# A heads' third key tile: its softmax weights turned by VectorE through DRAM instead of by TensorE, and half of the weight loads issued by ScalarE

## The chip, the cores and the metric

The kernel runs on one core of a Trainium2 chip. The core has a matrix engine (TensorE, "PE" in the profile, with its weight loads as "PEld"), VectorE ("DVE"), ScalarE ("ACT"), GpSimd ("POOL") and SyncE ("SP"), which here mostly issues DMA transfers. Each engine works through an instruction list of its own; semaphores order them against each other. The metric is device time in microseconds (us), the median of several executions.

## The reference

One layer of a hybrid decoder: 512 positions, 2048 channels, float32. An RMS-normalised input goes through one input projection `W_in`, whose columns feed three token mixers: A, dilated attention of 8 heads; B, a gated causal convolution with a layer norm; C, banded attention of 16 query heads. Their outputs side by side go through `W_out` and are added to the input. A second normalisation and a SwiGLU network follow. The part that the change touches is the softmax-weighted sum of A. Cut to what matters:

```
s = einsum(q, k) * hd**-0.5          # per head, key, query; masked
p = exp(s - m);  denom = sum(p)      # softmax weights
o = einsum(p, v) / denom             # weights times values
mix = softmax over three patterns' log-sum-exp, times o
out = concat(a, b, c) @ W_out + x
```

The scores have queries on partitions; the sum over keys wants the keys there. So the weights `p` must be turned (transposed) between the two matmuls.

## The kernel before, in words

**Projections in units.** `W_in` and `W_out` are worked off in 95 units of 1024 x 128 weights: units 0 to 62 are `W_in`, 63 to 94 `W_out`. A unit arrives by DMA (512 KB, tile `w`), is split by ScalarE into a rounded high part (`wh`, L295) and by VectorE into the rest (`wl`, L269), and TensorE forms three products for each of eight steps, 24 matmuls of 128x512: high by high, high by low, low by high (L328 to L330). `SPLIT_BUFS` = 3 pairs of high and low exist; the split runs `SPLIT_AHEAD` = 2 units ahead of use.

**Raw buffers and loads.** `pump` (L237) issues the load of the next unit as soon as a raw buffer is free; units 51 to 90 use five buffers, since others hold the turned softmax weights. The load overwrites a buffer whose last reader was the subtraction `wl` of an earlier unit. While `cooling` is on (the input projection), a buffer is released a unit later than its last reader is emitted; after that a load is emitted right behind the `wl` that frees its buffer. All these loads go through SyncE's queue, except the first four.

**Order of work.** It is written out: the kernel is scheduled by hand, so each engine does its instructions in the order in which the program emits them. Between the projection's matmuls a clock of ticks (`Ticks`, a few matmuls each) calls the steps that fell due: scores, exponentials, turns, weighing, taps of the convolution (L590), layer norm sums (`lns`, split into `lnh` and `lnl`, then averaged by TensorE as `lnm`, L617 and L618) and so on. The ticks are the same for both ways of turning.

**An A head.** TensorE writes the scores into three PSUM banks `a..s`; ScalarE scales them by the query norm (L941), VectorE adds the bias and takes the maxima (L946), ScalarE exponentiates (`a..e`, L954). Eight of the ten 128x128 blocks of weights (of key tiles 0, 1 and 3) are turned in 32x32 pieces by VectorE (`blocks_turn`, L971, tile `z`), written to DRAM (`ed`), read back rearranged (`et`, four transfers), and split into a high part (`ph`, ScalarE, L993) and a low part (`pl`, VectorE, L999). The blocks of the third key tile are turned by TensorE (`flip`, L1006) into a PSUM bank, and split from there (L1012, L1017). `weigh` then multiplies by the values. There are eight heads, named a0 to a3 with a 0 or 1 behind the tile's name; a0 and a1 are worked during the input projection, a2 and a3 during `W_out`.

Of the kernel before, what the change touches and what calls it, by code (L numbers as in the profile page):

```python
# [60 lines left out]
SPLIT_BUFS = 3  # L61
X_AHEAD = 8
SPLIT_AHEAD = 2
WARM = 8


# [55 lines left out]
def kernel(ctx: ExitStack, tc: tile.TileContext, xT, wi, wo, wgu, wd, cst_in, outT):  # L122
# [20 lines left out]
    def slot(name, dt=F32, cols=T):  # L143
        return sp.tile([P, cols], dt, name=name, tag="s")
# [96 lines left out]
    def pump(limit, most=99, eng=nc.sync):  # L241
        while at["entry"] < len(entries) and len(raws) < limit and entries[at["entry"]][0] not in held and most:
            most -= 1
            buf, key, parts = entries[at["entry"]]
            size = [part.shape[-1] * (part.shape[1] if len(part.shape) == 3 else 1) for part in parts]
            t, o = take(buf, key, sum(size)), 0
            for part, n in zip(parts, size):
                to = t[:, o:o + n]
                eng.dma_start(to.rearrange("p (n f) -> p n f", n=part.shape[1]) if len(part.shape) == 3 else to, part)
                o += n  # L250
            at["entry"] += 1

# [563 lines left out]
    def attention(kind, box, mix, mi, heads):  # L816
# [34 lines left out]
        def head(h):  # L851
# [104 lines left out]

            ph, pl = {}, {}

            def block(i, j):
                for u, un in enumerate(us):  # L960
                    for ii, k0, n, o in un:
                        if ii == i:
                            f = o + j * P - k0
                            return es[u][:, f:f + P]

            def blocks_turn():
                z = wp.tile([P, 1024], F32, name=f"{name}z{h}", tag=f"raw{TURN_BUFS[0]}", bufs=1)
                to = z.rearrange("p (j b q) -> p b j q", j=4, b=8)
                for u, c, bs in ((0, slice(0, 2), slice(0, 2)), (0, slice(2, 3), slice(4, 5)), (1, slice(0, 2), slice(2, 6, 3)),
                                 (2, slice(0, 2), slice(3, 7, 3)), (2, slice(3, 4), slice(7, 8))):  # L970
                    nc.vector.transpose(to[:, bs], es[u].rearrange("p (b j q) -> p b j q", b=NT, j=4)[:, c])  # L971
                ticks.after(2, blocks_leave, z)

            def blocks_leave(z):
                d = tc.dram_tile([P, 1024], F32, name=f"{name}ed{h}")
                nc.sync.dma_start(d, z)
                ticks.after(3, blocks_back, d)

            def blocks_back(d):
                turned[0] = 3 - turned[0]  # L980
                t = wp.tile([P, 1024], F32, name=f"{name}et{h}", tag=f"raw{TURN_BUFS[turned[0]]}", bufs=1)
                for j in range(4):
                    nc.sync.dma_start(t[32 * j:32 * j + 32].rearrange("p (i c) -> p i c", i=4),
                                      d.rearrange("(i p) c -> p i c", i=4)[:, :, j * 2 * P:(j + 1) * 2 * P])
                ticks.after(5, blocks_high, t.rearrange("p (i b q) -> p b i q", i=4, b=8))

            def queries4(t):
                return t.rearrange("p (b i q) -> p b i q", b=NT, i=4)

            def blocks_high(src):  # L990
                for t in range(2):
                    ph[t] = slot(f"{name}ph{h}{t}", F32R)
                    nc.scalar.copy(queries4(ph[t]), src[:, NT * t:NT * t + NT])  # L993
                ticks.after(EV, blocks_low, src)

            def blocks_low(src):
                for t in range(2):
                    pl[t] = slot(f"{name}pl{h}{t}", F32R)
                    nc.vector.tensor_sub(queries4(pl[t]), src[:, NT * t:NT * t + NT], queries4(ph[t]).bitcast(F32))  # L999

            def flip(t):
                b = bank(f"{name}t{h}{t}")
                o = 0
                for j, i0, i1 in TBANKS[kind][t]:
                    for i in range(i0, i1 + 1):
                        nc.tensor.transpose(b[:, o:o + P], block(i, j), ident)  # L1006
                        o += P
                ticks.after(ev, high, t, b, o)

            def high(t, b, o):  # L1010
                ph[t] = slot(f"{name}ph{h}{t}", F32R)
                nc.scalar.copy(ph[t][:, :o], b[:, :o])  # L1012
                ticks.after(EV, low, t, b, o)

            def low(t, b, o):
                pl[t] = slot(f"{name}pl{h}{t}", F32R)
                nc.vector.tensor_sub(pl[t][:, :o], b[:, :o], ph[t][:, :o].bitcast(F32))  # L1017

            def weigh():
                b = bank(f"{name}o{h}")  # L1020
# [41 lines left out]
            if kind == "c":  # L1062
                ticks.after(tu, packed_exps)
                ticks.after(tu + s2, packed_norm)
                ticks.after(tu + 1, packed_turn)
            else:
                ticks.after(tu + s2, invert, h, den)
                ticks.after(tu + 2, blocks_turn)
                ticks.after(tu + s2 + fl + 2, flip, 2)
            ticks.after(t0 + at_v, weigh)  # L1070
            if h == 1:
                ticks.after(t0 + at_v - 2, sums_back)
# [720 lines left out]
```

## Time and profile before

| | us |
|---|---|
| median of 3 runs | 1826.89 (1826.79 to 1827.04) |
| the profiled execution's own time | 1827.03 |
| its span | 1825.3 |
| TensorE busy in the span | 1818.3 |
| VectorE, ScalarE, GpSimd busy | 1434.5, 1327.6, 1022.1 |
| input projection and mixers | 0 to 375 of the span |
| `W_out` | 375 to 562 |
| SwiGLU up and down | 562 to 1825 |

The profile's clock runs from the span's start; rows of a timeline give start and duration. Granted TensorE clock is 0.999. Busy times of matmuls overlap (each row's end is modelled), so what a matmul costs is read from the distance between starts. A row's bracket gives the engine's idle time before it and what ended that. A DMA row on SP or ACT is the issue alone.

### The profile page before, as it was taken

What the parts mean: (1) busy time and instruction counts of PE and PEld (TensorE: products, weight loads), DVE (VectorE), ACT (ScalarE), POOL (GpSimd) and SP (SyncE); (2) the same over time, 40 slices, a digit from 0 to 9 for tenths busy, and PEclk for the clock granted to TensorE, in tenths of its full rate; (3) what the DMA queues carried; (4) which work ended last, traced back from release to release, by engine and by line L of the source; (5) the groups of instructions that cost most, each with busy time, mean ns of one, the idle gap of its engine ahead of it and who ended that gap; (6) DMA issues with size and microseconds to landing.
All of it is one profiled execution on the core that took longest, in us unless ns stands there. A gap on an engine that the chain in (4) does not pass through costs nothing.

```text
span 1825.3 us, 26570 instructions
## 1 busy us (share of the span) xinstructions
PE 1818.3 (100%) x8191; PEld 1509.9 (83%) x8191; DVE 1434.5 (79%) x1996; ACT 1327.6 (73%) x1848; POOL 1022.1 (56%) x793
## 2 busy tenths in 40 slices
PE   9999999999999999999999999999999999999998
PEld 7888888888888888888888888888888888888887
DVE  6779999987689777777777777777777777777777
ACT  6345656664468778888888888888887778877775
POOL 0116555120014577786887868878775568775652
PEclk9999999999999999999999999999999999999999
DMA  7355456666343557787777877778687579877645
GB/s 279 96 161 157 152 172 182 195 211 214 130 145 113 130 142 206 191 222 192 194 205 191 220 192 197 204 190 223 176 278 261 195 230 293 259 256 255 231 127 105
DMA packets 409295, 354.61 MB, mean 194 GB/s; under 512 B 177088, under 2 KB 331840, under 8 KB 409152
## 3 DMA queue, kind: packets, MB, share of 16 engines
q1 hardware_dynamic: 408576, 352.12, 65.7%
q8 instruction: 65, 1.06, 0.2%
q10 hardware_dynamic: 576, 0.79, 0.1%
q14 instruction: 78, 0.64, 0.1%
HBM read 270.00 MB, written 74.41 MB: 189 GB/s over the span
## 4 chain that ended last, share of the span: by engine, by line
PE 99%; DVE 1%; DMA 0%; issue 0%; ACT 0%; SPq 0%; DVEq 0%; ACTq 0%
PE out L1374 15%; PE out L1375 15%; PE out L1372 15%; PE out L1637 7%; PE out L1639 7%; PE out L1638 7%; PE o L328 3%; PE o L330 3%; PE o L329 3%; PE cq L328 2%; PE cq L329 2%; PE cq L330 2%; PE ak L328 1%; PE aq L328 1%; PE av L328 1%; PE ak L330 1%
## 5 line engine op out<-in xcount | busy, mean ns | idle before, releaser
L1372 PE MATMUL out<-wh,h 128*128 128x512 f32 x1232 | 479.2, 389 | 0.0
L1374 PE MATMUL out<-wl,h 128*128 128x512 f32 x1232 | 479.2, 389 | 0.0
L1375 PE MATMUL out<-wh,h 128*128 128x512 f32 x1232 | 479.2, 389 | 0.0
L1372 PEld LDWEIGHTS out<-wh,h 128*128 128x128 f32 x1232 | 231.2, 188 | 48.1
L1374 PEld LDWEIGHTS out<-wl,h 128*128 128x128 f32 x1232 | 231.2, 188 | 48.1
L1375 PEld LDWEIGHTS out<-wh,h 128*128 128x128 f32 x1232 | 231.2, 188 | 47.9
L1637 PE MATMUL out<-wh,a 128*128 128x512 f32 x620 | 240.4, 388 | 0.0
L1638 PE MATMUL out<-wl,a 128*128 128x512 f32 x620 | 240.3, 388 | 0.0
L1639 PE MATMUL out<-wh,a 128*128 128x512 f32 x620 | 240.3, 388 | 0.0
L295 ACT CAST wh<-w 128x1024 fp32r<-128x1024 f32 (+2 forms) x94 | 97.0, 1032 | 115.8 <-PE o L329 48.9
L1647 DVE TENSOR_TENSOR y<-y,out 128x512 f32<-128x512 f32 x192 | 128.6, 684 | 47.6 <-PE out L1639 46.1
L269 DVE TENSOR_TENSOR wl<-w,wh 128x1024 fp32r<-128x1024 f32 (+2 forms) x95 | 114.1, 1203 | 30.0 <-ACT wh L295 28.9
L1639 PEld LDWEIGHTS out<-wh,a 128*128 128x128 f32 x620 | 116.4, 188 | 24.0
L1638 PEld LDWEIGHTS out<-wl,a 128*128 128x128 f32 x620 | 116.4, 188 | 23.8
L1637 PEld LDWEIGHTS out<-wh,a 128*128 128x128 f32 x620 | 116.4, 188 | 23.8
L590 DVE SCALAR_TENSOR_TENSOR y<-bu,cst,y 128x511 f32<-128x511 f32 (+14 forms) x120 | 89.8, 748 | 0.5
L328 PE MATMUL o<-mh_c,wh 128*128 128x512 f32 x128 | 50.3, 393 | 0.0
L328 PE MATMUL cq<-hh,wh 128*128 128x512 f32 x128 | 50.0, 391 | 0.0
L329 PE MATMUL cq<-hl,wh 128*128 128x512 f32 x128 | 49.9, 390 | 0.0
L329 PE MATMUL o<-ml_c,wh 128*128 128x512 f32 x128 | 49.9, 390 | 0.0
L330 PE MATMUL o<-mh_c,wl 128*128 128x512 f32 x128 | 49.9, 390 | 0.0
L330 PE MATMUL cq<-hh,wl 128*128 128x512 f32 x128 | 49.8, 389 | 0.0
(2359 smaller groups left out, 4736.4 us busy)
## 6 DMA issues: line engine op xcount, KB each, us to landing
od<-a SPq DMA_DIRECT2D x154, 256.0 KB
a<-od SPq DMA_DIRECT2D x154, 256.0 KB
w<-in_wi SPq DMA_DIRECT2D x58, 512.0 KB
w<-in_wo SPq DMA_DIRECT2D x32, 512.0 KB
x<-in_xT SPq DMA_DIRECT2D x16, 256.0 KB
xr<-in_xT SPq DMA_DIRECT2D x16, 256.0 KB
x2d<-xr SPq DMA_DIRECT2D x16, 256.0 KB
z<-x2d SPq DMA_DIRECT2D x64, 64.0 KB
```

The source lines that it names most:

```text
L269: fn(*args)
L295: (nc.vector.tensor_copy if u == 0 else nc.scalar.copy)(hi[:, :n], t[:, :n])
L328: nc.tensor.matmul(out, wh, xh, start=start, stop=False)
L329: nc.tensor.matmul(out, wh, xl, start=False, stop=False)
L330: nc.tensor.matmul(out, wl, xh, start=False, stop=stop)
L1372: nc.tensor.matmul(b, x[:, high], wh[:, s], start=c == f == 0 and q in (7, 1, 5, 2), stop=False, skip_group_check=True)
L1374: nc.tensor.matmul(b, x[:, high], wl[:, s], start=False, stop=False, skip_group_check=True)
L1375: nc.tensor.matmul(b, x[:, low], wh[:, s], start=False, stop=c == f == 1, skip_group_check=True)
L1637: nc.tensor.matmul(b[:, lo:hi], x[:, high], wh[:, s], start=start, stop=False, skip_group_check=True)
L1638: nc.tensor.matmul(b[:, lo:hi], x[:, high], wl[:, s], start=False, stop=False, skip_group_check=True)
L1639: nc.tensor.matmul(b[:, lo:hi], x[:, low], wh[:, s], start=False, stop=last, skip_group_check=True)
L1647: getattr(eng, op)(t, t, src)
```

## The change

It does two things.

First, in A heads the third key tile's two blocks take the same way as the other eight: VectorE turns them into a second tile `z2`, SyncE writes it to DRAM (`ec`, 128 KB) and reads it back by four transfers (`eu`, 32 KB each), and `blocks_high` and `blocks_low` split three sources instead of two. TensorE's transposes (`flip`) and the split from PSUM (`high`, `low`) are gone. The ticks of the remaining steps stay.

Second, the loads of units 46 to 94 are issued by ScalarE's queue (`nc.scalar`) instead of SyncE's, at the same places of the program.

```diff
--- before.py
+++ after.py
@@ -61,6 +61,7 @@
 SPLIT_BUFS = 3
 X_AHEAD = 8
 SPLIT_AHEAD = 2
+ACT_LOADS = 46
 WARM = 8
 
 
@@ -246,7 +247,8 @@
             t, o = take(buf, key, sum(size)), 0
             for part, n in zip(parts, size):
                 to = t[:, o:o + n]
-                eng.dma_start(to.rearrange("p (n f) -> p n f", n=part.shape[1]) if len(part.shape) == 3 else to, part)
+                by = nc.scalar if isinstance(key, int) and key >= ACT_LOADS else eng
+                by.dma_start(to.rearrange("p (n f) -> p n f", n=part.shape[1]) if len(part.shape) == 3 else to, part)
                 o += n
             at["entry"] += 1
 
@@ -956,65 +958,52 @@
 
             ph, pl = {}, {}
 
-            def block(i, j):
-                for u, un in enumerate(us):
-                    for ii, k0, n, o in un:
-                        if ii == i:
-                            f = o + j * P - k0
-                            return es[u][:, f:f + P]
-
             def blocks_turn():
                 z = wp.tile([P, 1024], F32, name=f"{name}z{h}", tag=f"raw{TURN_BUFS[0]}", bufs=1)
                 to = z.rearrange("p (j b q) -> p b j q", j=4, b=8)
                 for u, c, bs in ((0, slice(0, 2), slice(0, 2)), (0, slice(2, 3), slice(4, 5)), (1, slice(0, 2), slice(2, 6, 3)),
                                  (2, slice(0, 2), slice(3, 7, 3)), (2, slice(3, 4), slice(7, 8))):
                     nc.vector.transpose(to[:, bs], es[u].rearrange("p (b j q) -> p b j q", b=NT, j=4)[:, c])
-                ticks.after(2, blocks_leave, z)
-
-            def blocks_leave(z):
+                z2 = slot(f"{name}z{h}", cols=2 * P)
+                to = z2.rearrange("p (j b q) -> p b j q", j=4, b=2)
+                for n in range(2):
+                    nc.vector.transpose(to[:, n], es[n + 1][:, 2 * P:3 * P].rearrange("p (j q) -> p j q", j=4))
+                es.clear()
+                ticks.after(2, blocks_leave, z, z2)
+
+            def blocks_leave(z, z2):
                 d = tc.dram_tile([P, 1024], F32, name=f"{name}ed{h}")
                 nc.sync.dma_start(d, z)
-                ticks.after(3, blocks_back, d)
-
-            def blocks_back(d):
+                d2 = tc.dram_tile([P, 2 * P], F32, name=f"{name}ec{h}")
+                nc.sync.dma_start(d2, z2)
+                ticks.after(3, blocks_back, d, d2)
+
+            def blocks_back(d, d2):
                 turned[0] = 3 - turned[0]
                 t = wp.tile([P, 1024], F32, name=f"{name}et{h}", tag=f"raw{TURN_BUFS[turned[0]]}", bufs=1)
                 for j in range(4):
                     nc.sync.dma_start(t[32 * j:32 * j + 32].rearrange("p (i c) -> p i c", i=4),
                                       d.rearrange("(i p) c -> p i c", i=4)[:, :, j * 2 * P:(j + 1) * 2 * P])
-                ticks.after(5, blocks_high, t.rearrange("p (i b q) -> p b i q", i=4, b=8))
-
-            def queries4(t):
-                return t.rearrange("p (b i q) -> p b i q", b=NT, i=4)
-
-            def blocks_high(src):
-                for t in range(2):
+                t2 = slot(f"{name}eu{h}", cols=2 * P)
+                for j in range(4):
+                    nc.sync.dma_start(t2[32 * j:32 * j + 32].rearrange("p (i c) -> p i c", i=4),
+                                      d2.rearrange("(i p) c -> p i c", i=4)[:, :, j * 64:(j + 1) * 64])
+                b8 = t.rearrange("p (i b q) -> p b i q", i=4, b=8)
+                ticks.after(5, blocks_high, (b8[:, :NT], b8[:, NT:], t2.rearrange("p (i b q) -> p b i q", i=4, b=2)))
+
+            def by_query(t, src):
+                return t[:, :src.shape[1] * P].rearrange("p (b i q) -> p b i q", i=4, q=32)
+
+            def blocks_high(srcs):
+                for t, src in enumerate(srcs):
                     ph[t] = slot(f"{name}ph{h}{t}", F32R)
-                    nc.scalar.copy(queries4(ph[t]), src[:, NT * t:NT * t + NT])
-                ticks.after(EV, blocks_low, src)
-
-            def blocks_low(src):
-                for t in range(2):
+                    nc.scalar.copy(by_query(ph[t], src), src)
+                ticks.after(EV, blocks_low, srcs)
+
+            def blocks_low(srcs):
+                for t, src in enumerate(srcs):
                     pl[t] = slot(f"{name}pl{h}{t}", F32R)
-                    nc.vector.tensor_sub(queries4(pl[t]), src[:, NT * t:NT * t + NT], queries4(ph[t]).bitcast(F32))
-
-            def flip(t):
-                b = bank(f"{name}t{h}{t}")
-                o = 0
-                for j, i0, i1 in TBANKS[kind][t]:
-                    for i in range(i0, i1 + 1):
-                        nc.tensor.transpose(b[:, o:o + P], block(i, j), ident)
-                        o += P
-                ticks.after(ev, high, t, b, o)
-
-            def high(t, b, o):
-                ph[t] = slot(f"{name}ph{h}{t}", F32R)
-                nc.scalar.copy(ph[t][:, :o], b[:, :o])
-                ticks.after(EV, low, t, b, o)
-
-            def low(t, b, o):
-                pl[t] = slot(f"{name}pl{h}{t}", F32R)
-                nc.vector.tensor_sub(pl[t][:, :o], b[:, :o], ph[t][:, :o].bitcast(F32))
+                    nc.vector.tensor_sub(by_query(pl[t], src), src, by_query(ph[t], src).bitcast(F32))
 
             def weigh():
                 b = bank(f"{name}o{h}")
@@ -1066,7 +1055,6 @@
             else:
                 ticks.after(tu + s2, invert, h, den)
                 ticks.after(tu + 2, blocks_turn)
-                ticks.after(tu + s2 + fl + 2, flip, 2)
             ticks.after(t0 + at_v, weigh)
             if h == 1:
                 ticks.after(t0 + at_v - 2, sums_back)
```

How this moves instructions, at the places of which the prediction speaks. In the change, lines 251 to 958 stand two lower on the page than before (L295 is now L297), and those from 1020 on eleven or twelve higher up (L1085 is now L1073). ScalarE's list around the cast of unit 66, before (`wh66` is the cast of unit 66, `a2s` the scaling of scores, `a2e` an exponential, `mh_a0` the high part of a finished head):

```order
L295 CAST wh66_4390<-w66_4111 128x1024
L954 ACTIVATE a2e02_4399,a2d0_4001<-a2s02_4333,a2d0_4001 128x512
L941 ACTIVATE a2s10_4401<-a2s10_4401,aq2r_4232 128x128
L941 ACTIVATE a2s10_4401<-a2s10_4401,aq2r_4232 128x256
L941 ACTIVATE a2s11_4432<-a2s11_4432,aq2r_4232 128x384
L295 CAST wh67_4449<-w67_4183 128x1024
L954 ACTIVATE a2e10_4459,a2d1_4002<-a2s10_4401,a2d1_4002 128x128
L954 ACTIVATE a2e10_4459,a2d1_4002<-a2s10_4401,a2d1_4002 128x256
L941 ACTIVATE a2s12_4463<-a2s12_4463,aq2r_4232 128x512
L954 ACTIVATE a2e11_4483,a2d1_4002<-a2s11_4432,a2d1_4002 128x384
L1085 CAST mh_a0_4486<-mix_a0_3827 128x512
```

And with the change:

```order
L251 DMA w70_4416<-in_wo 128x1024
L297 CAST wh66_4418<-w66_4135 128x1024
L956 ACTIVATE a2e02_4427,a2d0_4021<-a2s02_4361,a2d0_4021 128x512
L943 ACTIVATE a2s10_4429<-a2s10_4429,aq2r_4260 128x128
L943 ACTIVATE a2s10_4429<-a2s10_4429,aq2r_4260 128x256
L943 ACTIVATE a2s11_4463<-a2s11_4463,aq2r_4260 128x384
L251 DMA w71_4478<-in_wo 128x1024
L297 CAST wh67_4480<-w67_4209 128x1024
L956 ACTIVATE a2e10_4490,a2d1_4022<-a2s10_4429,a2d1_4022 128x128
L956 ACTIVATE a2e10_4490,a2d1_4022<-a2s10_4429,a2d1_4022 128x256
L943 ACTIVATE a2s12_4494<-a2s12_4494,aq2r_4260 128x512
L956 ACTIVATE a2e11_4516,a2d1_4022<-a2s11_4463,a2d1_4022 128x384
```

The loads of units 70 and 71 now stand ahead of the casts of 66 and 67, and everything on ScalarE stands behind them.

VectorE's list from the subtraction of unit 65 to that of unit 66 with the change (`a2z0` are the turned weights of one head; L966 is L971 of the kernel before):

```order
L271 TENSOR_TENSOR wl65_4349<-w65_4055,wh65_4348 128x1024
L1154 TENSOR_TENSOR xr0_4341<-xr0_4341,o0_0_4345 128x512
L830 RECIPROCAL weights_sums1_564<-a2d0_4021 128x4
L966 STREAM_TRANSPOSE a2z0_4452<-a2e00_4357 128x2x4x32
L966 STREAM_TRANSPOSE a2z0_4452<-a2e00_4357 128x4x32
L966 STREAM_TRANSPOSE a2z0_4452<-a2e01_4387 128x2x4x32
L966 STREAM_TRANSPOSE a2z0_4452<-a2e02_4427 128x2x4x32
L966 STREAM_TRANSPOSE a2z0_4452<-a2e02_4427 128x4x32
L970 STREAM_TRANSPOSE a2z0_4458<-a2e01_4387 128x4x32
L970 STREAM_TRANSPOSE a2z0_4458<-a2e02_4427 128x4x32
```

The two L970 rows, into a second tile of the same name, are new; the other rows stood there in this order.

ScalarE's list from the cast of unit 74 to the layer norm's `lnh`, before:

```order
L295 CAST wh74_4905<-w74_4642 128x1024
L1012 CAST a3ph12_4924<-a3t12_4914 128x256
L295 CAST wh75_4959<-w75_4716 128x1024
L609 CAST lnh_4969<-lns_4932 128x512
L993 CAST a3ph10_4974<-a3et1_4890 128x512
```

And with the change:

```order
L251 DMA w78_4962<-in_wo 128x1024
L297 CAST wh74_4964<-w74_4687 128x1024
L251 DMA w79_5009<-in_wo 128x1024
L297 CAST wh75_5011<-w75_4757 128x1024
L611 CAST lnh_5021<-lns_4986 128x512
L1000 CAST a3ph10_5026<-a3et1_4944 128x512
L1000 CAST a3ph11_5028<-a3et1_4944 128x512
L1000 CAST a3ph12_5030<-a3eu1_4949 128x256
```

The copy `a3ph12` from PSUM has gone behind the two others, and the loads of units 78 and 79 stand ahead of the casts of 74 and 75.

## The prediction

> **What bounds the kernel now.** I read the page's busy times and chain first, then TensorE's waits, then the stretch of the changed work on each engine.
>
> ```profile
> PE 1818.3 (100%) x8191; PEld 1509.9 (83%) x8191; DVE 1434.5 (79%) x1996; ACT 1327.6 (73%) x1848; POOL 1022.1 (56%) x793
> PE 99%; DVE 1%; DMA 0%; issue 0%; ACT 0%; SPq 0%; DVEq 0%; ACTq 0%
> PE idle L354 <- DVE nhalf L360: 1.1, 1, 1.1
> PE sides L1602 <- DVE y L1616: 1.1, 2, 0.6
> ```
>
> TensorE (PE) is the chain, and waits 2.2 us in all, none of it here. So the change can win only what its removed matmuls cost on PE, and can lose whatever newly makes PE wait. The profiled execution took 1827.03 us: span 1825.3 and 1.7 around it, 0.14 above the median 1826.89. 0.2% is 3.65 us, about what a measurement can tell from no change.
>
> **The removed transposes.** Each head loses two PE transposes, sixteen in all.
>
> ```profile
> 315.83 0.38 PE L1006 MATMUL a0t<-ident,a0e 128*128 128x128 f32 x2
> 315.97 0.47 PE L328 MATMUL ak<-hh,wh 128*128 128x512 f32 x1
> 316.29 0.39 PE L329 MATMUL ak<-hl,wh 128*128 128x512 f32 x1
> 316.51 0.40 PE L330 MATMUL ak<-hh,wl 128*128 128x512 f32 x1
> ```
>
> Ordinary matmuls start 0.22 to 0.23 apart. From the pair's start (315.83) to the second matmul behind it (316.29) pass 0.46, of which one matmul explains 0.23: a pair costs 0.23 us, eight cost **1.8 us**. (Were the pair's 0.38 busy all its own, it would be 3.0 us: the gain's upper end, still under 0.2%.)
>
> **What takes their place.** VectorE (DVE) turns two more 128x128 pieces per head; ScalarE (ACT) copies the third high part from SBUF, where it now copies from PSUM; DVE subtracts likewise.
>
> ```profile
> L971 DVE STREAM_TRANSPOSE a2z<-a2e x10: 269/402/414, 386.9 to 398.9; 128x256 f32<-128x256 f32 x6, 128x128 f32<-128x128 f32 x4
> ```
>
> Two of the 0.27 us form, pipelined, are about 0.45 us per head (3.6 in all). The third tile's copy and subtraction stay, and move behind those of the other two tiles; by the next rows, where two of 512 columns take 1.29, one of 256 is an estimated 0.4. Weighing keeps its tick:
>
> ```profile
> 367.29 1.29 DVE L999 TENSOR_TENSOR a1pl<-a1et,a1ph 128x512 fp32r<-128x512 f32 x2
> 371.39 0.39 PE L1030 MATMUL a1o<-a1ph,av 128*128 128x512 f32 x1
> ```
>
> Low parts end 2.8 us before PE's first weighing matmul in the tightest head; the third adds 0.4 to DVE and 0.4 to ACT, so this costs nothing; without that cover it would be up to 0.8 us per head.
>
> A sentence by itself: the Trainium skill, "VectorE: DVE Perf Modes", section "Rules for kernel authors", advises TensorE for a 128x128 transpose where PSUM will do, which is what the kernel before does. By durations this trace agrees (0.23 us per pair on PE against some 0.45 on DVE); on that page's rule the swap would be worth a loss wherever DVE's time is what PE waits for, which is the forecast's case below.
>
> **The loads that move.** 49 loads of 512 KB (units 46 to 94) leave SyncE's (SP's) queue for ACT's.
>
> ```profile
> L249 SPq DMA_DIRECT2D w<-in_wo x32: 328/360/1634, 337.5 to 510.8; - x32
> 0.80 1.86 ACTq L249 DMA_DIRECT2D w<-in_wi  x4
> SPq L249 <- DVE wl L269: 45.9, 15, 10.0
> 365.55 1.22 DVE L269 TENSOR_TENSOR wl<-w,wh 128x1024 fp32r<-128x1024 f32 x1
> 376.21 0.39 PE L330 MATMUL o<-mh_c,wl 128*128 128x512 f32 x1
> 350.00:400.00 50.00, 50.00 (x236) 41.94 (x235) 44.45 (x89) 33.26 (x67) 9.41 (x7) 1.00 0.73 208
> 400.00:450.00 50.00, 50.00 (x235) 41.76 (x234) 39.11 (x74) 25.41 (x49) 0.00 (x0) 1.00 0.67 212
> ```
>
> The first row gives 0.36 us per issue on SP, the second 0.46 on ACT; I take 0.4, 20 us in all. SP in turn issues five new transfers per head, 40 in all: at 0.36 some 14 us against 18 that it gives up. The third (SP's waits from 215 to 515 us) shows the load waiting 45.9 us for VectorE's low parts, 15 times: a load may not start until its buffer's last reader, the subtraction `wl`, has ended. On SP these waits held up only SP. On ACT, which works its instructions off in order, casts and exponentials stand behind them. The window rows (PE, PEld, DVE, ACT, POOL) show DVE 89% and ACT 67% busy from 350 to 400.
>
> Loads of units 46 to about 69 find that subtraction long done; they cost ACT 0.4 each beside the slack of the low parts: unit 63's is done at 366.8 (row of 365.55) and PE reads it at 376.2. Without that slack PE would lose 0.4 per unit. From unit 70 on the load of unit u+5 waits for `wl` of unit u and stands just ahead of the cast of unit u+1, which DVE needs for its next subtraction: a **lockstep** of ACT and DVE. I follow it with these rows (ACT, then DVE, then PE):
>
> ```profile
> 383.08 1.05 ACT L295 CAST wh<-w 128x1024 fp32r<-128x1024 f32 x1
> 384.03 0.68 ACT L954 ACTIVATE a2e<-a2s,a2d 128x512 f32<-128x512 f32 x1
> 392.66 0.61 ACT L1085 CAST mh_a<-mix_a 128x512 fp32r<-128x512 f32 x1
> 385.12 1.22 DVE L269 TENSOR_TENSOR wl<-w,wh 128x1024 fp32r<-128x1024 f32 x1
> 386.85 0.17 DVE L828 RECIPROCAL weights_sums<-a2d 128x4 f32<-128x4 f32 x1
> 389.66 1.22 DVE L269 TENSOR_TENSOR wl<-w,wh 128x1024 fp32r<-128x1024 f32 x1
> 394.36 1.22 DVE L269 TENSOR_TENSOR wl<-w,wh 128x1024 fp32r<-128x1024 f32 x1
> ```
>
> - Unit 65's `wl` ends at 386.3. Load 70 is then issued (386.7), the cast of 66 runs until 387.8 instead of 384.1, the exponential behind it until 388.6. DVE's reciprocal, at 386.85 before, waits for that: 1.75 late. With the two added turns (0.45) `wl` of 66 ends at 393.1, not 390.9: 2.2 late.
> - Load 71 waits for 393.1; cast 67 ends at 394.6; behind it two exponentials, a scaling, a third exponential and the cast `mh_a` (2.9 us together) end near 397.4, which DVE's `ml_a` right ahead of its next subtraction needs. `wl` of 67 ends at 399.2, not 395.6: 3.6 late.
> - The same way unit for unit it is about 4.5 late at 68, 6 at 70, 7 at 72. What PE loses on the way it does not lose again below, where I reckon by the clock time of ACT and DVE, so nothing is added here.
> - Where it bites is the layer norm, whose sums follow in the same two queues:
>
> ```profile
> 431.23 1.22 DVE L269 TENSOR_TENSOR wl<-w,wh 128x1024 fp32r<-128x1024 f32 x1
> 435.54 1.22 DVE L269 TENSOR_TENSOR wl<-w,wh 128x1024 fp32r<-128x1024 f32 x1
> 438.05 1.05 ACT L295 CAST wh<-w 128x1024 fp32r<-128x1024 f32 x1 [3.56 <-PE o L329]
> 439.01 0.61 ACT L609 CAST lnh<-lns 128x512 fp32r<-128x512 f32 x1
> 439.65 0.69 DVE L610 TENSOR_TENSOR lnl<-lns,lnh 128x512 fp32r<-128x512 f32 x1 [2.77 <-ACT lnh L609]
> 443.63 0.39 PE L618 MATMUL lnm<-lnl,one 128*128 128x512 f32 x1
> ```
>
> `wl` of 73 would end near 439.6 (7.1 late: issue and cast 1.5 after 432.1, three casts `a3ph`, then `mix_a`, `mh_a`, `ml_a` in turn on both engines), `wl` of 74 at 443.6. Then load 79, the cast of 75 (until 445.0), `lnh` (445.6) and `lnl` (446.3), which PE wanted at 443.6. PE resumes **2.7 us** later than in the old clock time; the 1.8 us gain, all earned before 434, is already inside that figure.
>
> After that PE and DVE are late together, so only relative lateness counts. Once more, at the gate's activation:
>
> ```profile
> 458.21 1.05 ACT L295 CAST wh<-w 128x1024 fp32r<-128x1024 f32 x1
> 458.94 1.22 DVE L269 TENSOR_TENSOR wl<-w,wh 128x1024 fp32r<-128x1024 f32 x1
> 466.21 1.22 DVE L269 TENSOR_TENSOR wl<-w,wh 128x1024 fp32r<-128x1024 f32 x1
> 469.68 0.39 PE L330 MATMUL o<-mh_c,wl 128*128 128x512 f32 x1
> ```
>
> Cast 78 now waits behind load 82 for 460.2: 2.4 late, and with it the activations and `wl` of 78 (467.4 to 469.5 at least) against PE at 469.68. That is 0 if DVE arrives as before and about 1.8 if it comes 2 us late into unit 77; I take 1.0. **Sum:** 2.7 + 1.0 = +3.7, so 1830.7 for the profiled execution and 1830.6 for the median; the forecast's own range is +1.8 to +5.5.
>
> **Rivals.** *No stall.* The loads' waits are found over, because SP, freed of them, lets the weights' round trip through DRAM and the other operands land earlier:
>
> ```profile
> SPq L983 <- DMA a2ed<-a2z: 11.1, 2, 5.7
> ```
>
> SP waits 11.1 us for the round trips of one pair of heads, partly because 512 KB loads travel with them. DVE idles (2.77 us before `lnl`), which could absorb a lag under 3 us. Then only the transposes go: 1826.89 - 1.8 = **1825.1**. Against it: DVE's 89%, and the order that puts each wait ahead of the next cast.
>
> The Trainium skill, "DMA: Bandwidth & Descriptors", section "Issuing engines are not separate DMA queues", says that issuing from several engines saves only the sequencer's issue time. By it the moved loads win nothing in transfer, and as SP's issue time is not in the chain (SPq 0%), this rival's time would be the best possible; no run yet shows the ACT side of it.
>
> *The queues hold each other.* SP's transfers also wait for earlier transfers' landings, of weight loads too (first row):
>
> ```profile
> SPq L760 <- DMA w<-in_wo: 2.6, 2, 1.4
> 336.32 1.09 SPq L731 DMA_DIRECT2D ak2wide<-ak2e  x2
> 339.19 1.14 ACT L993 CAST a0ph<-a0et 128x512 fp32r<-128x512 f32 x2
> 1.23 3.43 DMA cst<-in_cst
> ```
>
> Now a load that ACT issues late can hold SP, and SP's next round trip ACT. The place is the key tile `ak2wide`: its second transfer goes out at 336.9, and the load of unit 63, which stands ahead of it in the program, now leaves ACT only behind the third `a0ph` copy, at 340.8. With 3.4 us to land, as the one transfer in the chain took (last row), SP goes on at 344.2, 7 us late; the next key tile fares alike at unit 65. Of these 7 I estimate 4 to be slack, so that the lockstep starts 3 us later and both its ends move by 3 or so: +7.7 at the most, **1834.6**. It decides from about 4 us of SP's delay on. For it: such waits exist already; against it: SP's are short, 1.4 at most.
>
> *The change does not do what it says.* The transposes' 0.23 us could be hidden already (weight loads, not matmuls, setting the pace): then no gain and, without stall, 1826.9. PE's start times speak against it.
>
> **How the numbers follow.** Lockstep, as summed: 0.42, about half of it over 1830.5; no stall 0.33; queues holding each other 0.20; no gain and no stall 0.05. Slower by over 0.2%: 0.22 + 0.20 + a little = 0.46; within 0.2%: 0.52; faster by over 0.2%: 0.02, since even 3.0 us of gain is under 3.65. The range runs from the no-stall case, 1824.9, to just beyond the queues' case, 1835.5.
>
> **What would show it.** Right: PE rows waiting at `lnm` (L617/L618) on ACT `lnh` or DVE `lnl`, 2 to 6 us; the group `ACTq` load waiting for DVE `wl` in place of SP's 45.9 us; `wl` of units 66 to 74 progressively later. The gain: no L1006 matmul rows, and 0.23 us less per head up to 434 us. Wrong: PE's waits still 2.2 us in all (no stall), or PE waiting first at a2's or a3's scores on `ak` or `aq` (queues). The forecast falls if DVE's `wl` stays near its old times, which needs its order to hold enough work between one subtraction and the next to cover ACT's issue and cast, 1.5 us.

## The result, and the profile after

The changed kernel takes 1849.51 us (median of 4 runs, 1848.94 to 1852.49) against 1826.84 for the kernel before (4 runs, 1826.44 to 1827.04): a ratio of 1.0128, with a 95% interval of 1.0110 to 1.0145. That is 22.7 us slower, where +3.7 was forecast.

The head of the changed kernel's page:

```profile
span 1848.0 us, 26608 instructions
PE 1823.3 (99%) x8175; PEld 1511.7 (82%) x8175; DVE 1437.8 (78%) x2012; ACT 1327.0 (72%) x1848; POOL 1025.4 (55%) x793
```

TensorE's waits in it (us in total, times, longest):

```profile
PE a2s L865 <- DMA aq<-aq2l: 9.2, 1, 9.2
PE o L330 <- DVE xr L1154: 7.4, 3, 3.6
PE idle L356 <- DVE nhalf L362: 1.1, 1, 1.1
PE sides L1590 <- DVE y L1604: 1.1, 2, 0.6
PE a1o L1019 <- ACT a1ph L1000: 0.3, 1, 0.3
PE lnm L619 <- ACT lnh L611: 0.3, 1, 0.3
```

Two waits are new and large. One stands at the first scores of head a2, on the transfer of the query's low part (`aq2l`); the other, three times, at the first matmul of an output unit, on VectorE's addition `xr`. The layer norm's wait, which carried the forecast, is 0.3 us (and 0.2 on `lnl`).

The waits sum to 17.9 us more than before, the removed transposes give back about 2, and still the span is 22.7 longer. Of the 6.8 us that this leaves, some 4.7 are in the granted clock. About 2 more stand at the same waits: by the starts of the matmuls, what follows a wait comes 0.1 to 0.3 us later than the idle time shown, since the rows of matmuls that follow closely overlap. Windows of the changed kernel (window, length, busy us and count of PE, PEld, DVE, ACT, POOL, granted clock, DMA share, GB/s):

```profile
360.00:370.00 10.00, 10.00 (x47) 8.28 (x47) 5.34 (x9) 3.79 (x8) 1.04 (x1) 1.00 0.69 210
370.00:380.00 10.00, 0.76 (x4) 0.49 (x3) 7.53 (x12) 5.84 (x12) 0.00 (x0) 0.77 0.84 200
380.00:390.00 10.00, 10.00 (x37) 8.51 (x38) 6.74 (x15) 4.13 (x9) 4.27 (x3) 0.71 0.99 272
390.00:400.00 10.00, 10.00 (x49) 8.39 (x48) 7.44 (x13) 6.31 (x16) 1.04 (x1) 1.00 0.33 110
...
490.00:500.00 10.00, 9.64 (x35) 7.81 (x36) 5.09 (x6) 2.10 (x2) 0.00 (x0) 0.83 0.31 107
```

From 380 to 390 TensorE is "busy" throughout, but does 37 matmuls where a full window holds 47 to 49. The 0.77, 0.71 and 0.83 are means: with the windows cut where the clock changes, it is full or half.

```profile
379.60:385.70 6.10, 6.10 (x19) 5.33 (x20) 5.65 (x9) 1.66 (x3) 2.95 (x3) 0.50 0.96 278
385.70:390.00 4.30, 4.30 (x20) 3.58 (x20) 1.49 (x6) 2.87 (x7) 1.32 (x1) 1.00 1.04 272
```

Half clock lasts here from 375.5 to 385.7 (TensorE waits until 379.6) and from 491.5 to 494.9.

Following the same matmul in both traces shows where the 22.7 us arise (start before, and how much later it starts after):

| matmul | before | later by |
|---|---|---|
| projection of `aq3`, first | 362.76 | 0.6 |
| scores of a2, first | 369.56 | 10.0 |
| output unit 63, first | 375.76 | 13.0 |
| layer norm `lnm` | 443.40 | 13.3 |
| output unit 75, first | 451.91 | 17.3 |
| output unit 78, first | 469.23 | 21.1 |
| output unit 79, first | 474.67 | 22.9 |

After unit 79 the distance stays at 22.9 to 561 us.

The first jump has its origin on SyncE. The transfer that the scores wait for leaves SyncE at (kernel before, then changed):

```profile
363.20 0.47 SPq L702 DMA_DIRECT2D aq<-aq2l  x1
```

```profile
377.12 0.47 SPq L704 DMA_DIRECT2D aq<-aq2l  x1
```

SyncE, freed of 49 loads, is 13.9 us later than before. The order of its transfers did not change; this one row serves below as the measure of SyncE's lateness. It is a rough one, from one profiled execution per kernel: `e1`, `e3` and `e10` below do the same up to this row and have it at 366.7, 366.9 and 368.1; the change and `e4` also do the same and have it at 377.1 and 373.6.

The jump at unit 75, on ScalarE, VectorE and TensorE of the changed kernel:

```profile
463.74 0.33 ACTq L251 DMA_DIRECT2D w<-in_wo  x1
464.12 1.05 ACT L297 CAST wh<-w 128x1024 fp32r<-128x1024 f32 x1 [5.34 <-DVE wl L271]
465.61 1.65 ACT L427 ACTIVATE lq<-y 128x512 f32<-128x512 f32 x3
...
462.45 1.20 DVE L271 TENSOR_TENSOR wl<-w,wh 128x1024 fp32r<-128x1024 f32 x1
466.25 2.28 DVE L428 TENSOR_TENSOR lnv<-lnv,lq 128x512 f32<-128x512 f32 x3 [2.59 <-ACT lq L427]
468.45 0.68 DVE L1154 TENSOR_TENSOR xr<-xr,o 128x512 f32<-128x512 f32 x1
...
469.19 0.50 PE L330 MATMUL o<-mh_c,wh 128*128 128x512 f32 x1 [3.12 <-DVE xr L1154]
```

The load at 463.74 waits for the subtraction that ends at 463.65. Behind it stand the cast and the squares `lq`; VectorE waits 2.59 us for those, and its `xr`, which empties the PSUM bank that TensorE wants for unit 75, stands behind. So TensorE waits not for an operand but for a free bank: there are two for the output units.

### The profile page after: what moved, and what is told of

Its sections match the earlier page's. It is cut to its first block, busy times and chain, and to the rows that moved or that the text cites. A ratio compares the mean times of both kernels' runs of the same rounds, so it can differ in the third digit from the quotient of the medians.

```text
span 1848.0 us, 26608 instructions
## 1 busy us (share of the span) xinstructions
PE 1823.3 (99%) x8175; PEld 1511.7 (82%) x8175; DVE 1437.8 (78%) x2012; ACT 1327.0 (72%) x1848; POOL 1025.4 (55%) x793
## 4 chain that ended last, share of the span: by engine, by line
PE 72%; DVE 1%; issue 0%; DMA 0%; ACT 0%; DVEq 0%
PE out L1360 15%; PE out L1362 15%; PE out L1363 15%; PE out L1627 7%; PE out L1625 7%; PE out L1626 7%; PE o L330 2%; PE o L332 2%; PE o L331 2%; DVE y L1635 0%; DVE wl L293 0%; DMA out_T<-z 0%; DVE z L1534 0%; DVE y L1604 0%; PE sides L1590 0%
## 5 line engine op out<-in xcount | busy, mean ns | idle before, releaser
L297 ACT CAST wh<-w 128x1024 fp32r<-128x1024 f32 (+2 forms) x94 | 96.9, 1031 | 135.4 <-PE o L331 30.9
```

Source lines behind the costliest of these rows:

```text
L297: (nc.vector.tensor_copy if u == 0 else nc.scalar.copy)(hi[:, :n], t[:, :n])
```

## The experiments

Theories. **Q**: the two queues hold each other (ScalarE's loads and SyncE's round trips wait for one another through shared semaphores and ScalarE's order); this was the forecast's second rival. **T**: the five added transfers per head make SyncE late. **S**: off SyncE's queue the 512 KB loads run beside the short round trips instead of behind them and slow them. **L**: the lockstep of ScalarE and VectorE from unit 70 on. Times are medians; each ratio is against the kernel before on the same chip. In code cuts `...` stands for what is left out.

### One part alone, and each half of the loads

`e1`: `ACT_LOADS = 99` in the changed kernel. `e2`: the kernel before with only this:

```diff
+ACT_LOADS = 46
...
-                eng.dma_start(to.rearrange(...) ..., part)
+                by = nc.scalar if isinstance(key, int) and key >= ACT_LOADS else eng
+                by.dma_start(to.rearrange(...) ..., part)
```

`e3`: `ACT_LOADS = 70` in the changed kernel. `e4`: the changed kernel with

```diff
-                by = nc.scalar if isinstance(key, int) and key >= ACT_LOADS else eng
+                by = nc.scalar if isinstance(key, int) and ACT_LOADS <= key < 70 else eng
```

> Only the third key tile's way is changed; all loads stay with SyncE. Theory Q (the two queues hold each other: TensorE's 9.2 us wait at a2's scores comes from ScalarE's loads and SyncE's round trips waiting for one another): no wait of TensorE over 1 us, the transposes' 1.8 us gained, 1825 to 1827. Rival T (the five more transfers per head on SyncE make the query operands late by themselves): TensorE waits 5 us or more at a2's scores, 1835 or more. If both parts are needed together: in between, and the loads alone (next kernel) fast as well.

> Only the loads of units 46 to 94 go to ScalarE's queue; TensorE still turns the third key tile. Theory Q: most of the loss is here, TensorE waiting 4 us or more at a2's scores and 3 to 8 us between 440 and 500; 1838 to 1848. Rival T: nothing at a2's scores, at most the lockstep of ScalarE and VectorE behind the layer norm, 1827 to 1834.

> The change with ScalarE's loads from unit 70 on alone (units 46 to 69 back on SyncE). Theory Q says that the wait at a2's scores goes, since it is made by loads 58 to 67, and that the lockstep's waits behind the layer norm stay: 3 to 8 us of waits, 1828 to 1834. Rival T: the wait at a2's scores stays, 1840 or more.

> The change with ScalarE's loads only of units 46 to 69 (70 to 94 back on SyncE). Theory Q: the wait at a2's scores stays at 5 to 10 us, with the lower granted clock behind it, and the waits at 469 and 483 shrink or go: 1835 to 1843. If the loss belonged to the lockstep from unit 70 on alone, this would be within 2 us of the kernel before.

| | median us | ratio (95%) | `aq2l` leaves SyncE |
|---|---|---|---|
| before (shared) | 1826.94 | 1 | 363.2 |
| e1, turn only | 1829.36 | 1.0015 (1.0005 to 1.0024) | 366.7 |
| e2, loads only | 1841.82 | 1.0081 (1.0064 to 1.0098) | 367.8 |
| e3, turn, loads from 70 | 1840.60 | 1.0075 (1.0060 to 1.0090) | 366.9 |
| e4, turn, loads 46 to 69 | 1839.02 | 1.0065 (1.0049 to 1.0082) | 373.6 |

TensorE's waits beside the two at start and end that every kernel has; `e1`:

```profile
PE o L330 <- ACT wh L297: 1.1, 1, 1.1
PE a2s L865 <- DMA aq<-aq2l: 0.8, 1, 0.8
PE o L330 <- DVE xr L1154: 0.7, 1, 0.7
```

`e2`:

```profile
PE o L330 <- DVE xr L1168: 9.3, 4, 3.6
PE a2s L865 <- DMA aq<-aq2l: 0.6, 1, 0.6
```

`e3`, with the two layer norm matmuls of its timeline:

```profile
PE o L330 <- DVE xr L1154: 9.2, 4, 3.6
PE a2s L865 <- DMA aq<-aq2l: 1.2, 1, 1.2
```

```profile
445.88 0.51 PE L619 MATMUL lnm<-lnh,one 128*128 128x512 f32 x1 [0.43 <-ACT lnh L611]
446.61 0.50 PE L620 MATMUL lnm<-lnl,one 128*128 128x512 f32 x1 [0.22 <-DVE lnl L612]
```

`e4`, with a window:

```profile
PE a2s L865 <- DMA aq<-aq2l: 8.4, 1, 8.4
PE o L330 <- DVE xr L1154: 1.2, 1, 1.2
```

```profile
370.00:380.00 10.00, 3.96 (x11) 3.33 (x12) 7.61 (x13) 4.47 (x8) 0.73 (x1) 0.50 0.83 203
```

With the turn in place the loss has two halves. Loads 46 to 69 make the wait at a2's scores (over `e1`, `e4` costs 9.7 us), loads 70 to 94 the waits at the output units (`e3`, 11.2); with the 2.4 of `e1` they make 23.3, against 22.7 measured. Each of these is uncertain by 2 to 3 us, so that they agree this closely is luck. `e1` met neither of its theories: slower by 2.4 us where Q had the transposes' gain, but with no wait over 1.1 us where T had 5. My expectation of `e2` missed on the place: its loss is not at a2's scores but at the output units. At a2's scores the loads alone leave SyncE 4.6 us late, the turn alone 3.5, either just short of or at what TensorE's slack holds (waits of 0.6 and 0.8); both together 10.4 in `e4` and 13.9 in the change. That is the reason why neither part alone shows the 9 us wait. Both together are more than the sum, 8.1; why is not shown. `e3` is 6.6 us above the upper end of its expectation; `e4` lies within its own.

### Does ScalarE matter for the first half? The loads on GpSimd

```diff
-                by = nc.scalar if isinstance(key, int) and key >= ACT_LOADS else eng
+                by = nc.gpsimd if isinstance(key, int) and key >= ACT_LOADS else eng
```

`e10` is the same with `ACT_LOADS = 70`.

> The change with the loads of units 46 to 94 on GpSimd's queue instead of ScalarE's. SyncE's and ScalarE's transfers take turns on eight shared semaphores, and each waits for the landing of the transfer that held its semaphore before; GpSimd's transfers use eight others, so that here no round trip on SyncE waits for a load, nor a load for a round trip. Theory Q (they hold each other by these semaphores, and ScalarE's order does the rest): TensorE waits under 1 us at a2's scores, under 2 us after 440, 1825 to 1829. If instead SyncE is late by its own five further transfers per head, or the engines of the DMA are the limit: the wait at a2's scores stays at 5 us or more, 1835 or more.

> The third key tile turned by VectorE, units up to 69 loaded by SyncE, units 70 to 94 by GpSimd, which has little to do there. Beside the same with ScalarE (1840.6) it tells whether ScalarE's order is the cause. Theory L (what stands behind a waiting load on ScalarE): TensorE's waits at the output projection fall from 9.2 us under 2 us, 1826 to 1830. If taking these loads from SyncE's queue is itself the cause, as the sharing theory has it for the earlier units: 1835 or more.

`e5`: 1839.40 us, ratio 1.0072 (1.0058 to 1.0086). `e10`: 1828.46, ratio 1.0007 (0.9998 to 1.0017). The largest waits of `e5` and its row of `aq2l`:

```profile
PE a2s L865 <- DMA aq<-aq2l: 11.2, 1, 11.2
PE c6s L865 <- DMA cq<-cq6l: 1.4, 1, 1.4
```

```profile
381.23 0.47 SPq L704 DMA_DIRECT2D aq<-aq2l  x1
```

Those of `e10`, and its window over the layer norm and the gate:

```profile
PE a2s L865 <- DMA aq<-aq2l: 2.4, 1, 2.4
```

```profile
440.00:500.00 60.00, 60.00 (x274) 49.89 (x274) 40.38 (x62) 28.22 (x43) 6.90 (x12) 1.00 0.45 145
```

Theory Q falls as the cause: with no load on ScalarE and no semaphore shared between loads and round trips (in the trace GpSimd's transfers signal eight others than SyncE's), the wait at a2's scores is 11.2 us and SyncE 18 us late. The change does have a wait of Q's kind on SyncE:

```profile
SPq L838 <- DMA w<-in_wi: 4.0, 1, 4.0
```

It begins at 292.8 and is largely made up for: 8 us on, at the first `ak1h`, SyncE is 1.7 us late in the change and 1.8 in `e5`, which has no such wait. For the second half the opposite holds: neither `e5` nor `e10` makes TensorE wait at any output unit. That loss belongs to ScalarE's order, as theory L has it.

### The size of the loads

From both kernels, `e8` from `e5`, `e9` from the change:

```diff
+                if isinstance(key, int) and ACT_LOADS <= key < 70:
+                    nc.gpsimd.memset(to[:, P:], 0.0)
+                    to, part = to[:, :P], (part if len(part.shape) == 2 else part.rearrange("p n f -> p (n f)"))[:, :P]
```

Seven eighths of the weights of units 46 to 69 are left out, and set to zero.

> As the kernel with GpSimd issuing the loads (TensorE waits 11.2 us at a2's scores), but of units 46 to 69 only the first eighth is transferred and the rest set to zero by GpSimd: seven eighths of these weights are left out of the result, the instructions and waits around them stay. Theory S (sharing: off SyncE's queue the 512 KB loads run beside SyncE's short round trips instead of behind them, and each round trip lands later): the round trips land as fast as with the loads on SyncE (the key scale's transfer 1.5 us after its issue instead of 2.8), the wait falls under 3 us, 1824 to 1830. Rival O (SyncE's own list, or the order on GpSimd, makes it late): the wait stays at 7 us or more, 1834 or more.

> The change with the same cut: of units 46 to 69 only an eighth is transferred, the rest zeroed by GpSimd, and ScalarE issues all loads from 46 on. Theory S: the wait of 9.2 us at a2's scores falls under 3 us; the lockstep behind it (units 70 on, full size) stays, about 9 us of waits: 1834 to 1841. Rival Q (ScalarE's order and the shared semaphores make the wait, whatever the size): the wait at a2's scores stays at 6 us or more, 1844 or more.

`e8`: 1824.98 us, ratio 0.9991 (0.9981 to 1.0000). `e9`: 1839.61, ratio 1.0068 (1.0053 to 1.0083). The row of `aq2l` in `e8`:

```profile
364.99 0.47 SPq L707 DMA_DIRECT2D aq<-aq2l  x1
```

and in `e9` with TensorE's largest waits:

```profile
365.99 0.47 SPq L707 DMA_DIRECT2D aq<-aq2l  x1
```

```profile
PE o L333 <- DVE xr L1157: 8.6, 4, 3.6
PE a2s L868 <- DMA aq<-aq2l: 1.1, 1, 1.1
```

With every transfer and its wait in its place, 24 more `memset` on GpSimd, and an eighth of the bytes, SyncE is 16 us earlier in `e8` than in `e5`, 11 us earlier in `e9` than in the change, and the wait goes. So the bytes of the moved loads make SyncE late. The same bytes on SyncE's own queue (`e1`) do not: bytes and queue together are the cause, as theory S says. Nor do the loads leave at other times: where SyncE falls behind, from 305 to 335 us, units 58 to 62 are issued in `e5` and in the change within 3.7 us of `e1`. By the traces' semaphore events, the rearranged reads `et` of a0 and a1 land on average 3.6 us after the end of their issue in `e1`, 5.3 in `e5`, 4.3 in the change, 3.1 and 2.7 in `e8` and `e9`; but the key scales' `ak2d` and `ak3d` do not show the same order (1.4, 2.8, 1.3, 1.8, 1.4), so which transfers lose how much stays open. What is shown is size and queue; that the reason is the order within a queue (the load behind the round trip on one queue, beside it on two) is argued.

### The lockstep: the load behind the next cast

The kernel `e3`, but a load is emitted right after the next unit's cast instead of right after the subtraction that frees its buffer:

```diff
         split_up_to(u + SPLIT_AHEAD)
+        key = entries[at["entry"]][1] if at["entry"] < len(entries) else None
+        if lows and late_lows and not cooling and isinstance(key, int) and key >= ACT_LOADS:
+            pump(RAW_BUFS, 1)
```

(with the former place left out for these units, and buffers whose subtraction is not yet emitted kept closed).

> As the kernel with ScalarE's loads from unit 70 on (1840.6), but each load stands one cast later: load u+5, which waits for VectorE's subtraction of unit u, stands behind ScalarE's cast of unit u+1 instead of ahead of it. Theory L (lockstep: what stands behind a waiting load on ScalarE makes TensorE wait 9.2 us between 385 and 480): by the time ScalarE is there the subtraction is mostly over; TensorE's waits after 380 fall under 3 us, 1827 to 1832. If the loads' mere issue or their landing time is at fault: the waits stay near 9 us, 1838 or more.

1832.63 us, ratio 1.0035 (1.0021 to 1.0049), with the waits

```profile
PE o L339 <- DVE xr L1163: 4.4, 3, 2.2
PE a2s L874 <- DMA aq<-aq2l: 2.6, 1, 2.6
```

One place further back in ScalarE's list halves the waits at the output units (9.2 to 4.4) and returns 8 us. Less than expected: exponentials and copies still stand behind the load. Together with `e10`, where they are gone, the place of the load on ScalarE is the cause.

### The turn's own loss: its new transfers on GpSimd

`e1` with

```diff
-                nc.sync.dma_start(d2, z2)
+                nc.gpsimd.dma_start(d2, z2)
...
-                    nc.sync.dma_start(t2[32 * j:32 * j + 32]..., ...)
+                    nc.gpsimd.dma_start(t2[32 * j:32 * j + 32]..., ...)
```

> Only the third key tile's way is changed, all loads stay with SyncE, and the five new transfers per head are issued by GpSimd instead of SyncE. If the turn alone lost its 1.8 us to SyncE's longer list (theory S): TensorE's waits fall back to the 2.2 us of the kernel before, 1825 to 1826, a ratio of 0.999. If VectorE's added turns or the third copies' later place cost it: as with SyncE, 1828 to 1830.

1825.15 us, ratio 0.9996 (0.9987 to 1.0004): theory T for the turn's own part (what the expectation calls S is T here). `aq2l` leaves SyncE 2.2 us late, against 3.5 to 4.9 in `e1`, `e3` and `e10`, at

```profile
365.36 0.47 SPq L704 DMA_DIRECT2D aq<-aq2l  x1
```

and TensorE's waits are the old two and 0.9 us of small ones. Matmul by matmul TensorE goes from 0.3 us ahead of the kernel before (first scores of a0) to 1.7 ahead (layer norm), and keeps that. This is the best full version measured, but its interval includes 1: no win that this measurement can tell.

### What a wait costs beyond its length

The kernel before with one wait put in at output unit 87:

```diff
+        if half == 1 and n == OUT_ORDER[1][6]:
+            nc.gpsimd.tensor_copy(chain[0], t[:, :P])
+            for c in range(48):
+                nc.gpsimd.tensor_copy(chain[1 - c % 2], chain[c % 2])
...
+            if half == 1 and i == 8:
+                nc.tensor.transpose(b[:, :P], chain[0], ident)
```

> The kernel before with one wait of TensorE put in on purpose: at the output projection's 25th unit a transpose, whose result is overwritten, waits for a chain of 49 small copies on GpSimd that starts when VectorE has added up the 23rd unit. It asks what a wait costs beyond its own length. Theory C (after a long wait the granted clock of TensorE is lowered for some microseconds, as the changed kernel shows at 0.77 and 0.71): the span grows by the wait and 2 to 5 us more, and the window behind the wait shows a granted clock under 0.9 and fewer matmuls. Rival: the low clock in the changed kernel has another cause (the load of transfers, or the number of busy engines): the span grows by the wait alone, within 1 us, and the clock stays 1.00.

1845.97 us, ratio 1.0102 (1.0085 to 1.0119). The wait and the windows around it:

```profile
PE o L1235 <- POOL chain L1171: 16.2, 1, 16.2
```

```profile
510.00:520.00 10.00, 8.28 (x37) 6.53 (x35) 8.59 (x17) 5.66 (x13) 5.61 (x13) 1.00 0.41 125
520.00:530.00 10.00, 0.00 (x0) 0.00 (x0) 3.88 (x7) 0.89 (x2) 8.54 (x24) 0.66 0.46 139
530.00:540.00 10.00, 5.55 (x14) 4.40 (x15) 0.00 (x0) 0.00 (x0) 3.65 (x13) 0.50 0.00 0
540.00:550.00 10.00, 10.00 (x45) 8.22 (x44) 5.35 (x11) 5.48 (x11) 0.00 (x0) 0.98 0.24 73
```

The wait ends at 534.45. In the 5.55 us that remain of its window 14 matmuls run, about half of what 46 per 10 us make; the clock is granted at 0.50, and at full again from about 540. The same matmul stands 16.4 us later than before at the wait's end and 19.2 one unit on: 2.8 us on top of the wait. The DMA share is 0.00 in that window, so a crowd of transfers is not needed for the low clock.

How long a wait must be for this, the other traces tell only in part. In `e10` the wait of 2.4 us at a2's scores, which ends at 370.4, already has it:

```profile
370.00:376.80 6.80, 6.36 (x20) 5.52 (x21) 5.45 (x9) 1.48 (x3) 3.63 (x3) 0.50 0.88 280
376.80:386.00 9.20, 9.20 (x42) 7.65 (x41) 4.14 (x11) 8.33 (x20) 1.75 (x2) 1.00 0.86 242
```

That costs 3.0 us, more than the wait. The 2.6 us of `e6` are followed by half clock too (1.6 us lost), and of three waits of 3.1 us one is (`e9`), two are not (the change, `e3`). Behind waits up to 2.3 us (`e2`, `e3`, `e6`) the clock stays full. So neither the threshold nor the price goes by the length of the wait alone. What is lost is in each case about half of the time at half clock that lies behind the wait's end.

## Why the prediction was wrong

The sum had two terms, 2.7 us at the layer norm and 1.0 at the gate. It failed at three steps. It gave SyncE's chain no lateness, having weighed only the issues (some 14 us against 18); the chain was 13.9 us late, and that cost TensorE 12.4 us at a2's scores, the wait and the clock behind it. The 1.0 was in truth 9.0, since TensorE needed a free bank and not only an operand. And no wait was priced at more than its length.

**The direction and the gain were right.** TensorE lost more than the transposes gave. Their 1.8 us came out as predicted: in `e1` TensorE gains 1.1 us over the first four heads, in `e7` 1.4 over all eight beside some 0.4 of small waits.

**"The queues hold each other", the rival with 0.20, was the nearest to what happened, and three terms of it failed.** Its sign appeared: TensorE waits first at a2's scores, on `aq`. I put SyncE 7 us late with 4 us of slack. The slack was about right (waits of 0.6 and 0.8 at 3.5 to 4.6 us of lateness); the lateness was 10.1 at the place that I named (the second `ak2wide` at 346.9) and 13.9 at `aq2l`. Its +7.7 was not what its own terms give either (3.7 and 3 make 6.7). I let the excess delay only the lockstep's start, and overlooked that TensorE itself needs `aq2l` next: it waited 9.2 us there. And the mechanism was another: not waiting on one another's semaphores but the loads' bytes on a second queue (`e5`, `e8`, `e9`). The load of unit 63 did leave ScalarE at 341.6, as reckoned (340.8); but in `e5` it leaves GpSimd at 333.9, earlier than before, and the second `ak2wide` is still 11.3 us late. My chain from `ak2wide` took for granted that a round trip keeps its landing time when the loads leave its queue.

**"Some 14 us against 18 that it gives up": SyncE's added transfers were costed at nothing.** I compared issue times. But SyncE also waits for landings, in order (11.1 us in the row that the prediction shows), so five more transfers per head can delay what follows them, and giving up the loads did not make up for it. `e1` against `e7`: 4.0 us in the medians, each taken against its own kernel before; all of the turn's gain and more.

**The lockstep was read correctly up to the layer norm, and then the wrong need was followed.** I had `lnl` ready at 446.3; in `e3`, where the earlier loads stay with SyncE, TensorE reads it at 446.61. The steps agree less closely: the low parts of units 66 and 67 end there at 394.7 and 400.5 (393.1 and 399.2 reckoned), those of 73 and 74 at 439.6 and 443.9 (439.6 and 443.6), so the closeness at the end is partly luck. But I asked only when TensorE needs each low part and `lnl`. It also needs an empty PSUM bank for each output unit, and the addition `xr` that empties one stands in VectorE's list among the work that the lockstep delays. "What PE loses on the way it does not lose again" was right (in `e3` unit 66 starts 2.8 us late, and `lnm` then 2.5), but "+1.0" for all that follows was not: unit 75 waits 3.1 us and unit 78 3.6, and TensorE falls 9.0 us further behind with the clock's share.

**No term for the clock.** The sum priced a wait at its own length. Of the 22.9 us, 3.0 come between the end of the wait at a2's scores and output unit 63, and 1.75 between units 78 and 79, at half clock; `e11` shows the price on its own. The Trainium skill warns of this: "TensorE: Matmul & The Clock Gate", section "Why this matters for your kernels", advises against gaps of TensorE over some 3 us, behind which the clock falls to half. The runs agree on the half (0.50 in `e4`, `e10` and `e11`), but not on the 3 us as a limit: half clock followed waits of 2.4 and 2.6 us too, and did not follow two of 3.1.

The no-stall rival gave 1825.1, which is what `e7` (1825.15) measures, with all loads left on SyncE and the new transfers off it; the interval of `e7` is 1.6 us to either side, so the last tenth is luck. The sentence from the Trainium skill that I set beside it ("DMA: Bandwidth & Descriptors", section "Issuing engines are not separate DMA queues": the transfers interleave on the same engines, and only issue time is saved) was worth more than I made of it: I used it to say that nothing is won, and not to ask what loses when transfers interleave that stood in line before. No run here shows the interleaving itself.

## What to carry to other kernels

Before moving a transfer to another engine's queue, list everything that stands behind it on that engine and will wait for the transfer's own condition, and what its bytes will now run beside: a large load behind short round trips on one queue can be cheaper than the same load on a free queue. Follow all that the critical engine needs, the buffers that others must empty for it as well as its operands. Price a wait of a busy TensorE at more than its length: here waits from 2.4 us on cost up to 3 us more.

## What the runs showed of the hardware

- TensorE's granted clock was full or half (0.50 in `e11`, from 523.3 to 540.3). Half clock behind a wait of 16.2 us cost 2.8 us (`e11`), behind 9.2 us 3.0 and behind 3.6 us 1.75 (the change), behind 2.4 us 3.0 (`e10`), behind 2.6 us 1.6 (`e6`); behind 3.1 us nothing in the change and in `e3`.
- Of 24 loads of 512 KB taken off SyncE's queue, those issued by then made SyncE's chain of short transfers 10 to 18 us late where head a2's query leaves (373.6 in `e4`, 377.1 in the change and 381.2 in `e5` against 363.2). With an eighth of their bytes it was 11 us earlier on ScalarE (`e9`) and 16 on GpSimd (`e8`). Without the turn's added transfers the same loads made it 4.6 us late (`e2`).
